# RMSNorm inside a two-layer decoder trunk: the sum of squares and its spread on TensorE, written another way

## The chip, the cores and the metric

The kernel runs on one core of a Trainium2 chip. The metric is device time in microseconds (us) of one execution; several runs are given, and one further execution was profiled. The engines are named as in the profile: PE (TensorE matmul), PEld (its weight loads), DVE (VectorE), ACT (ScalarE), POOL (GpSimd) and SP (SyncE).

## The reference

A trunk of two layers on x of shape (1, 1024, 1024) in float32: a gated short convolution with a SwiGLU FFN, then dilated attention with a SwiGLU FFN, then a last norm. What matters here is the norm, which is taken five times, over the model dimension:

```python
def rms_norm(x, g):
    xf = x.astype(jnp.float32)
    y = xf * lax.rsqrt(jnp.mean(xf * xf, axis=-1, keepdims=True) + EPS)
    return (y * g.astype(jnp.float32)).astype(x.dtype)

def reference(x, mix_norm, ffn_norm, final_norm, ...):
    for i in range(DEPTH):                       # DEPTH = 2
        h = rms_norm(x, mix_norm[i])
        if i % N_MIXERS == 0:
            x = x + short_conv_mixer(h, ...)
        else:
            x = x + dilated_attention_mixer(h, ...)
        h = rms_norm(x, ffn_norm[i])
        x = x + swiglu(h, w_gate[i], w_up[i], w_down[i])
    return rms_norm(x, final_norm)
```

## The kernel before, in words

**Layout.** Activations are kept transposed: x is eight tiles X[0] to X[7] of 128 model dimensions by 1024 positions. A sum over the model dimension is thus a sum over partitions and over the eight tiles. A norm's factor 1/rms is one number per position, and where a tile is multiplied by it, it must stand in all 128 partitions: that is the tile `rstd`, 128 by 1024, the same row in every partition.

**Products.** Every float32 product is made of three matmuls of a type called fp32r in the program (F32R): an operand is split into a high part (a Copy on ACT into an F32R tile) and a low part (a subtraction on DVE, line 144 in `split`, 565 for activations), and high times high, high times low and low times high are added in a PSUM bank. The weights are combined and split while the kernel runs (a Strassen scheme: sums of weight blocks, the "combos", line 191; seven products m = 1 to 7 per unit u). A unit's product is twelve matmuls of 512 columns, lines 572 to 574; the plain products are lines 371 to 373.

**Order.** The schedule is written by hand: each engine runs its instructions in the order in which the program emits them. After each product the program calls `start(n)` or a hook, and what is emitted there stands at that place in every engine's queue. `ensure(k)` emits the weight sums and splits up to the k-th operand; `combos[key, u](m)` emits weight sums alone. Small tiles of 512 columns come from a pool of 20 ("half pages", `half_page`).

**The norm.** `Norm` gathers squares of the X tiles in `acc` (128 by 1024, still to be summed over partitions). `stats(c0, c1)` is a generator in two steps. First step: for each 128 positions a plain float32 matmul with `acc` as weights and one column of ones gives the sums with positions on partitions (line 472); ACT takes a Sqrt (475), DVE a reciprocal (476), giving `r`, and DVE multiplies an identity by r into a diagonal tile of 512 columns (481). Second step: a plain float32 matmul of a tile of ones with the diagonal puts r in all partitions (488), and ACT copies the bank into `rstd` (489). The three callers:

- The convolution and the query and key projection (`mix`) take 1024 positions at once: the first step as `gather`, the second as `spread`, some units later. In the convolution the square of rstd is taken (1108) and applied on DVE (980). In the query and key projection `r` is kept for attention, where the value tiles are scaled by it with positions on partitions (1517).
- An FFN takes two halves of 512. The first belongs to `group1`, between the output tiles of the mixer's last product; the second is emitted in `start(n)` of `feed_forward`, the first step at n = key + 1 (key is 0 or 1 for the two FFNs), the second at n = key + 2. What follows is `second_half`, DVE's scaling of X by rstd (1278) and the splits of the result, and a small Silu (1366) that loads its table early.
- The last norm works in three pieces of 512, 256 and 256 positions, with its own `squared_sum` (1954, 1958, 1959, 1961) and `spread` (1969, 1982); the last piece's sum takes the last square as a term of its own (1956).

**Tables of ACT.** Sqrt, Silu, and Exp with Ln need different tables, and an ACT_TABLE_LOAD stands where the set changes. Some loads are put early by hand: a small Sqrt on a scratch tile at the end of attention (1695) and ahead of the last norm (1977), and a named set that holds Ln and Exp (LN_EXP) at the bias tables (530) and at attention's start (1812).

Of the kernel before, what the change touches and what calls it, by code (L numbers as in the profile page):

```python
# [17 lines left out]
S = 1024  # L18
# [81 lines left out]
def trunk(ctx: ExitStack, tc: tile.TileContext, x, gains_in, cwi, ck, cwo, wqkv, wo, relb,  # L100
# [24 lines left out]
    less = consts.tile([128, 5, KT], F32)  # L125
    taps = consts.tile([128, KT, 3], F32)
    ones = consts.tile([128, 128], F32)
    eye = consts.tile([128, 128], F32)
    eps = consts.tile([128, 1], F32)
    scratch = consts.tile([128, 1], F32)  # L130
# [265 lines left out]
    class Norm:  # L396
# [68 lines left out]
        def stats(self, c0, c1):  # L465

            self.flush()
            w = c1 - c0
            nt = w // 128
            b = bank()  # L470
            for t in range(nt):
                nc.tensor.matmul(b[:, t:t + 1], self.acc[:, c0 + 128 * t:c0 + 128 * t + 128], ones[:, 0:1],
                                 start=True, stop=True)
            r = self.r = consts.tile([128, KT], F32, name="r", tag="r", bufs=2)
            nc.scalar.activation(r[:, :nt], b[:, :nt], AF.Sqrt, scale=1.0 / D, bias=eps)
            nc.vector.reciprocal(r[:, :nt], r[:, :nt])
            diags = []
            for p0 in range(0, nt, 4):
                n = min(4, nt - p0)
                diag = half_page("diag")  # L480
                nc.vector.tensor_tensor(out=view(diag, 0, [[128, n], [1, 128]]),
                                        in0=view(eye, 0, [[0, n], [1, 128]]),
                                        in1=view(r, p0, [[1, n], [0, 128]]), op=ALU.mult)
                diags.append((c0 + 128 * p0, 128 * n, diag))
            yield
            for p0, n, diag in diags:
                b = bank()
                nc.tensor.matmul(b[:, :n], ones, diag[:, :n], start=True, stop=True)
                nc.scalar.activation(self.rstd[:, p0:p0 + n], b[:, :n], AF.Copy)

    def add_to_x(n, banks):
        for (c0, c1), b in banks.items():
# [377 lines left out]
    class Conv(Strassen):  # L870
# [182 lines left out]
        def mix(self, group1):  # L1053
# [48 lines left out]

            def gather():
                next(stats)

            def spread():
                run(stats)
# [14 lines left out]
    class QueryKey(Conv):  # L1122
# [43 lines left out]
        def mix(self):  # L1166
# [40 lines left out]

            def gather():
                next(stats)

            def spread():
                run(stats)
                self.ready = True

            def load():
# [21 lines left out]
    class Swiglu(Strassen):  # L1237
# [111 lines left out]
        def feed_forward(self, stats, last_step, after, final=None):  # L1349
            prep = []  # L1350

            def start(n):
                if n == 0:
                    last_step()
                    for m in (6, 7):
                        combos[self.key, 1](m)
                    ensure(self.at(3, 1))
                if n == self.key + 1:
                    next(stats)
                    combos[self.key, 2](6)  # L1360
                    ensure(self.at(0, 6))
                elif n == self.key + 2:
                    run(stats)
                    prep.append(self.second_half())
                    next(prep[0])
                    nc.scalar.activation(scratch, eps, AF.Silu)
                    ensure(self.at(1, 6))
                elif n == 4:
                    ensure(self.at(1, 7))
                elif n in (5, 7, 8, 10, 12):  # L1370
                    next(prep[0], None)
                if n in (8, 24):
                    self.ahead = 3 if n == 8 else 2

            self.run(start)
            key = ("d", self.key)
            if final:
                final(key, self.plain, self.hid)
                return
            for n in range(KT):  # L1380
                add_to_x(n, both(take(key + (n,), 2 if n > 3 else 1), self.plain, self.hid))
                after(n)
# [22 lines left out]
    def into_ffn(i, norm):  # L1405
# [10 lines left out]
        def group1(key, ks, acts):  # L1416
# [9 lines left out]
            def between(j, n):  # L1426
# [48 lines left out]
    def attention(norm, qk):  # L1475
# [193 lines left out]
        def finish(p):  # L1669
# [22 lines left out]
            yield  # L1692
            nc.scalar.activation(z[:, half(1)], z[:, half(1)], AF.Exp, scale=-1.0)
            scaled(1)
            nc.scalar.activation(scratch, eps, AF.Sqrt)
            yield
            last_part.append(rest)
            yield
# [110 lines left out]
                    add_to_x(n, {c: b})  # L1809

        X[:] = [None] * KT
        nc.scalar.preload_act_table_set(LN_EXP)
        bias = {0: load_bias(0)}
        load_kq(0)
        run(value_tiles(0, 0))
# [35 lines left out]


    nc.scalar.dma_start(gains, gains_in)

    def load_first():

# [53 lines left out]
    with tc.tile_pool(name="third", bufs=1) as scope["pool"]:  # L1910
# [5 lines left out]
        def final(key, ks, hid):  # L1916
# [55 lines left out]
            diags = []  # L1972

            def between(i, n):
                add_squares(int(n > 0))
                if (i, n) == (0, 5):
                    nc.scalar.activation(scratch, eps, AF.Sqrt)
                if i and n == 1:
                    diags.append(squared_sum(i - 1))
                elif i and n == 3:  # L1980
                    s = slice(*pieces[i - 1])
                    nc.scalar.activation(norm.rstd[:, s], spread(diags.pop()), AF.Copy)
# [67 lines left out]
```

## Time and profile before

| | |
|---|---|
| time, median of 3 runs | 2130.8 us (2130.04 to 2131.32) |
| time of the profiled execution | 2129.8 us |
| its span | 2128.0 us |
| granted TensorE clock, mean | 0.996 |
| PE busy | 2102.3 us (99%), 11082 matmuls |
| DVE busy | 1739.8 us (82%) |
| ACT busy | 1015.7 us (48%) |
| POOL busy | 234.4 us (11%) |

Times of the trace count from the span's start. A row of a timeline gives start, duration, engine, line, operation, tiles written and read, shapes and count; in brackets stands the idle time of the engine before it and what ended it. A float32 matmul that is not F32R has two records. Ends of matmuls are modelled, their starts are not, so PE's pace is read from one start to the next.

### The profile page before, as it was taken

What the parts mean: (1) busy time and instruction counts of PE and PEld (TensorE: products, weight loads), DVE (VectorE), ACT (ScalarE), POOL (GpSimd) and SP (SyncE); (2) the same over time, 40 slices, a digit from 0 to 9 for tenths busy, and PEclk for the clock granted to TensorE, in tenths of its full rate; (3) what the DMA queues carried; (4) which work ended last, traced back from release to release, by engine and by line L of the source; (5) the groups of instructions that cost most, each with busy time, mean ns of one, the idle gap of its engine ahead of it and who ended that gap; (6) DMA issues with size and microseconds to landing.
All of it is one profiled execution on the core that took longest, in us unless ns stands there. A gap on an engine that the chain in (4) does not pass through costs nothing.

```text
span 2128.0 us, 30922 instructions
## 1 busy us (share of the span) xinstructions
PE 2102.3 (99%) x11082; PEld 1806.5 (85%) x11082; DVE 1739.8 (82%) x3262; ACT 1015.7 (48%) x1861; POOL 234.4 (11%) x335
## 2 busy tenths in 40 slices
PE   9999999999999999999999999999999999999998
PEld 7888888888888888887899999888788888888887
DVE  8898769988888888878967687787998888888876
ACT  7333426443444554445545545554544444456435
POOL 1000000110101000010322322111011101001000
PEclk9999999999999999999999999999999999999999
DMA  7332642323333566351767767745223233358432
GB/s 219 94 94 70 228 134 75 104 100 109 114 101 108 162 208 211 108 168 40 250 208 186 182 182 211 216 164 152 64 85 109 101 108 114 105 195 241 157 95 79
DMA packets 141464, 300.78 MB, mean 141 GB/s; under 512 B 48188, under 2 KB 54414, under 8 KB 141312
## 3 DMA queue, kind: packets, MB, share of 16 engines
q1 hardware_dynamic: 107488, 201.94, 31.5%
q0 software_dynamic: 26192, 82.17, 11.9%
q10 hardware_dynamic: 7632, 14.70, 1.8%
q8 instruction: 88, 1.44, 0.3%
q14 instruction: 64, 0.52, 0.1%
HBM read 208.48 MB, written 82.93 MB: 137 GB/s over the span
## 4 chain that ended last, share of the span: by engine, by line
PE 85%; DVE 7%; ACT 3%; DMA 2%; issue 2%; POOL 1%; SPq 0%; DVEq 0%; ACTq 0%; POOLq 0%
PE bank L574 19%; PE bank L572 19%; PE bank L573 19%; PE bank L373 4%; PE bank L372 4%; PE bank L371 4%; PE bank L664 3%; PE bank L667 3%; PE bank L666 3%; PE bank L1642 2%; POOL mb L1623 1%; PE bank L1512 1%; PE bank L1513 1%; PE bank L1514 1%; DVE w L144 1%
## 5 line engine op out<-in xcount | busy, mean ns | idle before, releaser
L572 PE MATMUL bank<-b,w 128*128 128x512 f32 x1952 | 764.0, 391 | 2.2 <-ACT w L143 1.8
L574 PE MATMUL bank<-b,w 128*128 128x512 f32 x1952 | 762.0, 390 | 3.6 <-DVE w L144 3.5
L573 PE MATMUL bank<-b,w 128*128 128x512 f32 x1952 | 761.4, 390 | 0.4 <-DVE b L883 0.3
L574 PEld LDWEIGHTS bank<-b,w 128*128 128x128 f32 x1952 | 366.9, 188 | 83.9 <-DVE w L144 7.4
L572 PEld LDWEIGHTS bank<-b,w 128*128 128x128 f32 x1952 | 367.2, 188 | 78.9 <-ACT w L143 2.9
L573 PEld LDWEIGHTS bank<-b,w 128*128 128x128 f32 x1952 | 367.1, 188 | 76.3 <-DVE b L883 1.1
L143 ACT ACTIVATE w<-combo 128x512 fp32r<-128x512 f32 (+2 forms) x488 | 249.1, 540 | 230.2 <-DVE combo L191 213.3
L144 DVE TENSOR_TENSOR w<-combo,w 128x512 fp32r<-128x512 f32 (+2 forms) x488 | 277.7, 583 | 37.6 <-ACT w L143 36.9
L578 ACT ACTIVATE part<-bank 128x512 f32<-128x512 f32 x186 | 110.8, 596 | 390.0 <-PE bank L574 386.6
L144 DVE TENSOR_TENSOR w<-raw,w 128x512 fp32r<-128x512 f32 (+2 forms) x342 | 189.5, 576 | 37.5 <-ACT w L143 37.5
L582 DVE TENSOR_TENSOR part<-part,bank 128x256 f32<-128x256 f32 (+1 forms) x366 | 171.5, 500 | 31.1 <-PE bank L574 16.6
L143 ACT ACTIVATE w<-raw 128x512 fp32r<-128x512 f32 (+2 forms) x342 | 166.9, 530 | 44.4 <-PE bank L574 11.5
L371 PE MATMUL bank<-w_hi,w 128*128 128x512 f32 (+1 forms) x400 | 153.4, 384 | 3.8 <-ACT w_hi L143 3.7
L372 PE MATMUL bank<-w_lo,w 128*128 128x512 f32 (+1 forms) x400 | 149.8, 375 | 1.2 <-DVE w_lo L144 1.2
L373 PE MATMUL bank<-w_hi,w 128*128 128x512 f32 (+1 forms) x400 | 149.8, 375 | 0.7 <-DVE w L144 0.7
L493 DVE TENSOR_TENSOR x<-x,bank 128x512 f32<-128x512 f32 (+1 forms) x104 | 66.4, 644 | 62.6 <-PE bank L373 61.4
L802 DVE TENSOR_TENSOR x<-x,bank 128x512 f32<-128x512 f32 x136 | 93.2, 685 | 29.1 <-PE bank L574 29.1
L191 DVE TENSOR_TENSOR combo<-raw 128x512 f32<-128x512 f32 (+1 forms) x172 | 111.7, 649 | 0.0
L371 PEld LDWEIGHTS bank<-w_hi,w 128*128 128x128 f32 x400 | 75.8, 190 | 17.1 <-ACT w_hi L143 3.9
L372 PEld LDWEIGHTS bank<-w_lo,w 128*128 128x128 f32 x400 | 75.9, 190 | 14.9 <-DVE w_lo L144 2.0
L373 PEld LDWEIGHTS bank<-w_hi,w 128*128 128x128 f32 x400 | 75.6, 189 | 14.7 <-DVE w L144 1.6
L565 DVE TENSOR_TENSOR b<-hin,b 128x512 fp32r<-128x512 f32 x126 | 79.7, 689 | 9.3 <-ACT b L564 9.3
(243 smaller groups left out, 3467.1 us busy)
## 6 DMA issues: line engine op xcount, KB each, us to landing
hin<-part SPq DMA_DIRECT2D x126, 256.0 KB
raw<-in_ffn_w_gate SPq DMA_DIRECT2D x44, 512.0 KB
raw<-in_ffn_w_up SPq DMA_DIRECT2D x44, 512.0 KB
part<-sum POOLq DMA_DIRECT2D x72, 256.0 KB, 2.3
raw<-in_ffn_w_down SPq DMA_DIRECT2D x48, 384.0 KB
raw<-in_attn_w_qkv SPq DMA_DIRECT2D x27, 512.0 KB
raw<-in_conv_w_in SPq DMA_DIRECT2D x24, 512.0 KB
part<-part POOLq DMA_DIRECT2D x36, 256.0 KB, 2.4
```

The source lines that it names most:

```text
L143: nc.scalar.activation(hi, src, AF.Copy)
L144: eng.tensor_tensor(out=lo, in0=src, in1=hi, op=ALU.subtract)
L191: eng.tensor_tensor(out=c, in0=a, in1=b, op=op)
L371: nc.tensor.matmul(b, whi[:, a], ahi[:, s], start=first, stop=False)
L372: nc.tensor.matmul(b, whi[:, a], alo[:, s], start=False, stop=False)
L373: nc.tensor.matmul(b, wlo[:, a], ahi[:, s], start=False, stop=last)
L572: nc.tensor.matmul(b, hi[:, a], bhi, start=start and k == 0, stop=False, skip_group_check=True)
L573: nc.tensor.matmul(b, hi[:, a], blo, start=False, stop=False, skip_group_check=True)
L574: nc.tensor.matmul(b, lo[:, a], bhi, start=False, stop=k == n - 1, skip_group_check=True)
L578: nc.scalar.activation(t, b, AF.Copy)
L582: nc.vector.tensor_tensor(out=t, in0=t, in1=b, op=ALU.add)
L802: nc.vector.tensor_tensor(out=X[n][:, half(h)], in0=X[n][:, half(h)], in1=b, op=ALU.add)
```

## The change

The diff touches all norms but the last piece of the last one.

- `stats` becomes a generator of three steps: high parts of `acc` on ACT; low parts on DVE; then `spread_sums`, in which two F32R matmuls with a tile of ones (`ones_r`) as weights give the sum over partitions, in all partitions at once, and ACT takes Ln (with scale 1/D and eps) and Exp (with scale -1/2) into `rstd`.
- `gather` takes the first two steps at once. In the FFNs the first two steps are emitted with the two calls of `combos` (m = 6 and 7), so that the high parts stand ahead of one weight sum and the low parts behind it; for the second half this moves from n = key + 1 to n = 0.
- The value tiles' `r` is made by writing one row of `rstd` to DRAM and reading it back with positions on partitions, two DMAs on POOL's queue in the query and key projection's `spread`.
- The first two pieces of the last norm use `split` and `spread_sums`. The set LN_EXP is loaded at the start and ahead of the last norm; the loads at attention's start and end go; the Sqrt table is loaded behind the second piece's Exp for the last piece, which stays as it was.

```diff
@@ class Norm
         def stats(self, c0, c1):
 
             self.flush()
-            w = c1 - c0
-            nt = w // 128
-            b = bank()
-            for t in range(nt):
-                nc.tensor.matmul(b[:, t:t + 1], self.acc[:, c0 + 128 * t:c0 + 128 * t + 128], ones[:, 0:1],
-                                 start=True, stop=True)
-            r = self.r = consts.tile([128, KT], F32, name="r", tag="r", bufs=2)
-            nc.scalar.activation(r[:, :nt], b[:, :nt], AF.Sqrt, scale=1.0 / D, bias=eps)
-            nc.vector.reciprocal(r[:, :nt], r[:, :nt])
-            diags = []
-            for p0 in range(0, nt, 4):
-                n = min(4, nt - p0)
-                diag = half_page("diag")
-                nc.vector.tensor_tensor(out=view(diag, 0, [[128, n], [1, 128]]),
-                                        in0=view(eye, 0, [[0, n], [1, 128]]),
-                                        in1=view(r, p0, [[1, n], [0, 128]]), op=ALU.mult)
-                diags.append((c0 + 128 * p0, 128 * n, diag))
-            yield
-            for p0, n, diag in diags:
-                b = bank()
-                nc.tensor.matmul(b[:, :n], ones, diag[:, :n], start=True, stop=True)
-                nc.scalar.activation(self.rstd[:, p0:p0 + n], b[:, :n], AF.Copy)
+            parts = []
+            for p0 in range(c0, c1, HALF):
+                s = slice(p0, min(p0 + HALF, c1))
+                hi, lo = (half_page("sum", F32R) for _ in range(2))
+                nc.scalar.activation(hi, self.acc[:, s], AF.Copy)
+                parts.append((s, hi, lo))
+            yield
+            for s, hi, lo in parts:
+                nc.vector.tensor_tensor(out=lo, in0=self.acc[:, s], in1=hi, op=ALU.subtract)
+            yield
+            for s, *sums in parts:
+                spread_sums(self.rstd[:, s], sums)
+
+    def spread_sums(rstd, sums):
+        b = bank()[:, :rstd.shape[1]]
+        for i, t in enumerate(sums):
+            nc.tensor.matmul(b, ones_r, t, start=i == 0, stop=i == len(sums) - 1)
+        nc.scalar.activation(rstd, b, AF.Ln, scale=1.0 / D, bias=eps)
+        nc.scalar.activation(rstd, rstd, AF.Exp, scale=-0.5)
@@ Conv.mix and QueryKey.mix
             def gather():
                 next(stats)
+                next(stats)
@@ QueryKey.mix
             def spread():
                 run(stats)
+                rms = dram.tile([1, S], F32, name="rms")
+                norm.r = consts.tile([128, KT], F32, name="scales")
+                nc.gpsimd.dma_start(rms, norm.rstd[0:1, :])
+                nc.gpsimd.dma_start(norm.r, bass.AP(rms.tensor, rms.offset, [[1, 128], [128, KT]]))
                 self.ready = True
@@ Swiglu.feed_forward
                 if n == 0:
                     last_step()
                     for m in (6, 7):
+                        next(stats)
                         combos[self.key, 1](m)
                     ensure(self.at(3, 1))
                 if n == self.key + 1:
-                    next(stats)
                     combos[self.key, 2](6)
                     ensure(self.at(0, 6))
                 elif n == self.key + 2:
@@ into_ffn, group1
                 if n == i:
                     pre.append(norm.stats(0, HALF))
-                    next(pre[0])
                     for m in (6, 7):
+                        next(pre[0])
                         combos[i, 0](m)
@@ attention
-            nc.scalar.activation(scratch, eps, AF.Sqrt)
...
-        nc.scalar.preload_act_table_set(LN_EXP)
@@ the start
     nc.scalar.dma_start(gains, gains_in)
+    nc.scalar.preload_act_table_set(LN_EXP)
...
     nc.vector.memset(ones, 1.0)
+    nc.vector.memset(ones_r.bitcast(F32), 1.0)
@@ final
                 if (i, n) == (0, 5):
-                    nc.scalar.activation(scratch, eps, AF.Sqrt)
+                    nc.scalar.preload_act_table_set(LN_EXP)
                 if i and n == 1:
-                    diags.append(squared_sum(i - 1))
+                    s = slice(*pieces[i - 1])
+                    known.append(split(norm.acc[:, s], [half_page("sum", F32R)[:, :s.stop - s.start] for _ in range(2)]))
                 elif i and n == 3:
                     s = slice(*pieces[i - 1])
-                    nc.scalar.activation(norm.rstd[:, s], spread(diags.pop()), AF.Copy)
+                    spread_sums(norm.rstd[:, s], known.pop())
                     scale.extend((i - 1, k, norm.rstd[:, s]) for k in range(KT))
+                    if i == len(pieces) - 1:
+                        nc.scalar.preload_act_table(AF.Sqrt)
```

More of the change, by code (lines that the diff above doesn't have):

```diff
@@ L127, in trunk @@
     ones = consts.tile([128, 128], F32)
+    ones_r = consts.tile([128, 128], F32R)
     eye = consts.tile([128, 128], F32)
@@ L1355, in start @@
                     for m in (6, 7):
+                        next(stats)
                         combos[self.key, 1](m)
@@ L1970, in spread @@
                 return b[:, :w]
-            diags = []
+            known = []
             def between(i, n):
```

## The prediction, made before the changed kernel was run

> **What bounds the kernel now.** I read the page first, then busy time by stretch, then the timelines of PE, ACT and DVE around each of the five norms.
>
> ```profile
> span 2128.0 us, 30922 instructions
> PE 2102.3 (99%) x11082; PEld 1806.5 (85%) x11082; DVE 1739.8 (82%) x3262; ACT 1015.7 (48%) x1861; POOL 234.4 (11%) x335
> PE 85%; DVE 7%; ACT 3%; DMA 2%; issue 2%; POOL 1%; SPq 0%; DVEq 0%; ACTq 0%; POOLq 0%
> ...
> 352.00:400.00 48.00, 48.00 (x214) 39.76 (x213) 47.77 (x83) 26.91 (x48) 3.06 (x6) 1.00 0.25 82
> 1470.00:1520.00 50.00, 48.99 (x218) 39.99 (x217) 46.17 (x76) 33.77 (x59) 5.12 (x6) 1.00 0.30 74
> ```
>
> The first three lines are the span, the busy times and the chain's shares by engine: PE is busy 99% of the span and holds 85% of the chain. Less PE work therefore shortens the run wherever the engines that feed PE keep up. The two stretches (length, PE, PEld, DVE, ACT, POOL) show where that is in doubt: just behind the norm of each FFN, DVE is busy 47.77 of 48 and 46.17 of 50 us. The accounting is thus: PE time taken out, less what DVE and ACT cannot follow.
>
> **PE: what goes and what comes.** The norm of the convolution on PE's timeline, 1024 columns:
>
> ```profile
> 66.53 0.39 PE L574 MATMUL bank<-b,w 128*128 128x512 f32 x1
> 66.76 1.84 PE L472 MATMUL bank<-ones,acc 128*128 128x1 f32 x16
> ...
> 68.79 0.40 PE L573 MATMUL bank<-b,w 128*128 128x512 f32 x1
> ...
> 76.77 1.88 PE L488 MATMUL bank<-diag,ones 128*128 128x512 f32 x4
> ...
> 78.72 0.40 PE L573 MATMUL bank<-b,w 128*128 128x512 f32 x1
> ```
>
> Ends are modelled, so I go by starts. A 512-column matmul of high or low parts starts 0.23 us after the one before (66.53 to 66.76). The eight one-column products (sixteen records) hold PE from 66.76 until the L573 at 68.79, less the one L572 between, 68.79 - 66.76 - 0.23 = 1.80 us. The two fp32 spreads hold it 78.72 - 76.77 - 0.23 = 1.72 us. The new form has four products of high or low parts, 4 x 0.23 = 0.92 us (their type is that of L572, so I take that row's price). So 1.80 + 1.72 - 0.92 = 2.60 us of PE go per 1024 columns. Four norms have 1024 columns and the last one changes on 768: 4.75 x 2.60 = 12.4 us, the most that PE's work alone can give.
>
> **What ACT and DVE get.** Groups by line and form (busy us, mean ns):
>
> ```profile
> L143 ACT ACTIVATE w<-combo 128x512 fp32r<-128x512 f32 x248 | 150.9, 626 | 108.5 <-DVE combo L191 108.2
> L144 DVE TENSOR_TENSOR w<-combo,w 128x512 fp32r<-128x512 f32 x248 | 170.0, 688 | 30.9 <-ACT w L143 30.7
> L882 ACT ACTIVATE b<-x,gains 128x512 fp32r<-128x512 f32 x36 | 24.1, 717 | 36.1 <-DVE x L493 26.0 <-DMA oh<-in_one_hot 3.7 <-issue 3.2
> L1665 ACT ACTIVATE z<-bank 64x512 f32<-64x512 f32 x32 | 18.9, 591 | 17.4 <-PE bank L1642 16.9
> L1632 ACT ACTIVATE lp<-lp 128x512 f32<-128x512 f32 x16 | 9.8, 615 | 0.0
> L481 DVE TENSOR_TENSOR diag<-eye,r 128x512 f32<-128x512 f32 x8 | 5.4, 690 | 0.3
> L489 ACT ACTIVATE rstd<-bank 128x512 f32<-128x512 f32 x8 | 4.6, 596 | 10.4 <-PE bank L488 10.3
> ```
>
> Per 512 columns DVE exchanges the 0.69 us diagonal for a 0.69 us subtraction and loses a reciprocal: no dearer. ACT gets a high part (0.63), a Ln and an Exp (0.62) for a small Sqrt and a 0.60 copy. A Ln out of a bank with eps as operand isn't in the trace: L1665 without an operand is 0.59, L882 with one 0.72; I take 0.65, and about 0.06 more for Exp to wait for it. So rstd comes 0.73 us later behind its matmul than by the copy, in each half. ACT is 48% busy; this counts only where DVE waits for rstd.
>
> **Convolution: 2.6.** There DVE does wait:
>
> ```profile
> 77.83 0.60 ACT L489 ACTIVATE rstd<-bank 128x512 f32<-128x512 f32 x1 [4.09 <-PE bank L488]
> 80.41 0.69 DVE L980 TENSOR_TENSOR part<-part,acc 128x512 f32<-128x512 f32 x1 [2.75 <-ACT acc L1108]
> 87.15 0.39 PE L574 MATMUL bank<-b,w 128*128 128x512 f32 x1
> 82.35 0.69 DVE L144 TENSOR_TENSOR w<-combo,w 128x512 fp32r<-128x512 f32 x1
> ```
>
> PE reaches the spread 1.80 earlier and ends it 2.60 earlier; on ACT 2 x 0.73 = 1.46 us more stand ahead of L1108, so DVE resumes at least 1.1 earlier and loses at most 1.5 us on PE. The low part that ends at 82.35 + 0.69 is first read at 87.15, 4.1 us later: the lead covers it, and the whole 2.60 stays.
>
> **FFNs: 2.7 and 1.9.** The second half's norm, one row of FFN 0 (340), then FFN 1:
>
> ```profile
> 340.47 1.05 PE L472 MATMUL bank<-ones,acc 128*128 128x1 f32 x8 [0.24 <-DVE acc L446]
> ...
> 1493.87 1.02 PE L488 MATMUL bank<-diag,ones 128*128 128x512 f32 x2
> 1494.93 0.60 ACT L489 ACTIVATE rstd<-bank 128x512 f32<-128x512 f32 x1 [2.97 <-PE bank L488]
> 1495.56 2.50 DVE L1278 TENSOR_TENSOR x<-x,rstd 128x512 f32<-128x512 f32 x4 [1.25 <-ACT rstd L489]
> 1518.17 0.50 PE L574 MATMUL bank<-b,w 128*128 128x512 f32 x1 [1.01 <-DVE w L144]
> ```
>
> In FFN 1, PE reaches the spread earlier by the first half's 1.30 and the one-column products' 0.90: at 1491.67 instead of 1493.87. Two matmuls end about 0.6 later (second start, and its 0.39), at 1492.3; Ln and Exp give rstd at 1493.6, and DVE begins its scaling 1.9 us earlier than 1495.56. From there to 1518.17, where PE waited 1.01 us for a low part, DVE has work throughout: the 1470 to 1520 row leaves it 3.8 us idle in all, 1.25 of them in the row at 1495.56 itself and the rest ahead of it. PE would be there 2.6 earlier, DVE 1.9: the wait grows to 1.7, and 1.9 stays. High and low parts are now asked for at n = 0, two or three units ahead of the spread, so it finds them made; their subtraction stands behind one weight sum on DVE so that DVE doesn't stand idle for ACT's high part. FFN 0 runs the same list but its spread comes one unit earlier, twelve matmuls or 2.7 us: at the same place it has 2.7 - 1.01 = 1.7 us to spare, and the 352 to 400 row shows no idle PE. It loses 0.7 of that and keeps 2.6, with some 0.1 of the 0.24 us in which PE waited for the squares' sum.
>
> **Query and key: 1.9.**
>
> ```profile
> 981.97 1.28 ACT L475 ACT_TABLE_LOAD   x1
> 983.26 0.27 ACT L475 ACTIVATE r<-bank,eps 128x8 f32<-128x8 f32 x1
> 996.40 0.60 ACT L578 ACTIVATE part<-bank 128x512 f32<-128x512 f32 x1 [2.13 <-PE bank L574]
> 997.55 0.69 DVE L144 TENSOR_TENSOR w<-combo,w 128x512 fp32r<-128x512 f32 x1 [0.72 <-ACT w L143]
> 1001.89 0.60 ACT L578 ACTIVATE part<-bank 128x512 f32<-128x512 f32 x1 [1.67 <-issue]
> 1003.13 1.41 DVE L883 SCALAR_TENSOR_TENSOR b<-x,gains,b 128x512 fp32r<-128x512 f32 x2 [1.15 <-ACT b L882]
> 1019.04 0.50 PE L574 MATMUL bank<-b,w 128*128 128x512 f32 x1 [0.47 <-DVE w L144]
> ```
>
> At 1019.04 PE waits for DVE, which has worked without a pause since 1003.13. So what counts is how much earlier DVE comes. Its two pauses of 0.72 and 1.15 lie behind ACT copies (L578) that waited for PE; with PE 2.6 earlier both go, 1.87 together. The two ACT operations more at the spread (1.3 us) use room that the lost table load and earlier matmuls make ahead of it. I keep 1.9 of 2.6.
>
> **1/rms by way of DRAM.** Two DMAs are new on POOL's queue, and the second waits for the first. No row has 4-byte pieces, so their price is open upwards:
>
> ```profile
> part<-sum POOLq DMA_DIRECT2D x72, 256.0 KB, 2.3
> 1019.41 0.58 POOL L1146 DMA_DIRECT2D kq<-kq_hi  x1 [74.22 <-ACT w L143]
> 1093.34 1.28 ACT L1812 ACT_TABLE_LOAD   x1
> 1094.63 0.84 ACT L1517 ACTIVATE v<-bank,r 128x256 f32<-128x256 f32 x2
> ```
>
> By the first row (2.3 us from issue to landing) with 0.58 an issue, two in series are about 6 us. rstd is made ahead of the copy at 996.40; the first issue behind them on POOL comes at 1019.41, the first reader at 1094.63. Up to 23 us nothing stands behind them: nothing lost. Without that cover the key stores would wait, and with them attention's first loads.
>
> **Table loads.** The loads for the first and the third norm's Sqrt (981.97), at attention's start (1093.34) and at its end go; the one ahead of the last norm becomes one of Ln and Exp, and a Sqrt load is added ahead of the last piece. The row at 981.97 prices one at 1.28: the Sqrt starts 0.01 us behind its end. PE's waits name none of them, so they are worth nothing beyond what is counted here. The Trainium skill, "ScalarE: Activation LUTs", What ACT_TABLE_LOAD costs, gives about 2.66 us for a switch, drain included. The trace shows no such drain around the load (0.01 us). By that page the added load alone would be 1.38 dearer, an estimate, and the time about 2122.3.
>
> **The end: 0.8.**
>
> ```profile
> 2113.87 0.36 ACT L1982 ACTIVATE rstd<-bank 128x256 f32<-128x256 f32 x1
> 2115.06 0.42 ACT L1929 ACTIVATE sq<-x 128x256 f32<-128x256 f32 x1 [0.82 <-DVE x L493]
> 2118.45 0.42 ACT L1929 ACTIVATE sq<-x 128x256 f32<-128x256 f32 x1 [0.43 <-DVE x L493]
> ```
>
> 768 columns give PE 1.95, 1.30 of it ahead of this place. ACT then does Ln, Exp and a load where one copy stood: about 0.4 + 1.28 = 1.7 more. Free at 2114.23 before, it is free at 2114.23 - 1.30 + 1.7 = 2114.6; the squares of tiles 4 to 7 start 0.45 earlier than 2115.06 and, without the last 0.43 us of waiting, the last one 0.8 earlier. What follows it is unchanged.
>
> **Sum.** 2.6 + 2.7 + 1.9 + 1.9 + 0.8 = 9.9 us. The profiled run took 2129.8 us (span 2128.0 and 1.8 around it); it would take 2119.9 and span 2118.1. The runs' median, 2130.8, is 1.0 above it: **2120.9 us**. Attention gets no term: its waits follow from what arrives, and all of that arrives earlier alike. A small shift there is in the range.
>
> **Rivals.** (1) *All of PE's time carries*: DVE's leads are longer than the waits show. 12.4 gives 2118.4. For it: behind the convolution and FFN 0 PE shows no wait. Against it: at 1019 and 1518 it waits already, so there the lead is nil. (2) *ACT and DVE bind*: Ln and Exp come late at both FFNs and the table load holds the end. Convolution 2.0, FFNs 1.5 and 1.0, query and key 0.9, end 0.0: 5.4, 2125.4. For it: DVE's 47.77 of 48. (3) *The change doesn't get one table set*: Ln and Exp each load theirs, 2 x 1.28 more per spread. FFN 1 and the query and key lose 2.6 each, FFN 0 0.9 beyond its spare 1.7, the end 1.5: 2.3 left, 2128.5. Against it: attention's Exp and Ln (L1632, L1665) alternate through the slots behind L1812's one load. (4) *Slower: the pool of 20 half tiles runs full.* At an FFN's start there are 8 scaled columns, 8 weight sums, 2 saved products and 1 diagonal, 19 by the code; two parts for one diagonal make 20. A high part that must wait for a tile holds everything behind it on ACT, copies out of banks too, and PE then waits for a product's end, 2.7 us. At both halves of both FFNs, the convolution and the query and key that is 6 x 2.7 = 16.3 against 9.9: 2137.3. It decides from four places on. Against it: 20 still fit, and elsewhere there are fewer tiles. (5) *The added Sqrt load holds ACT for twice its 1.28 us*: the last square is then 0.5 late in place of 0.8 early, 8.6, 2122.2. Against it: the 0.01 us behind the load at 981.97.
>
> **How the numbers follow.** Forecast 0.64 (own range 2119 to 2122.5), rival 1 0.14, rival 2 0.11, rival 3 0.03, rival 4 0.05, rival 5 0.03. About 0.2% (4.3 us) is what a measurement here tells from none: faster by more is the forecast with rivals 1, 2 and 5, 0.92; within it is rival 3, 0.03; slower is rival 4, 0.05. The range goes from 2117.2 (rival 1 with a microsecond for attention) to 2125.4 (rival 2).
>
> **What would show it.** L472 and L488 gone from PE and PE's busy time about 12 us less; PE's wait near 1518 grown to about 1.7 and that near 1019 to about 1.2; no new PE wait in the convolution and behind FFN 0's norm; six ACT table loads instead of nine, no two within one norm; the value tiles never waiting for a DMA. Wrong would be: a PE wait at the new products themselves, ACT waiting at a high part for a tile, or PE waits behind the norms that sum to over 5 us.

## The result, and the profile after

| | before | changed |
|---|---|---|
| median of 5 runs | 2130.8 us (2129.76 to 2131.7) | 2121.44 us (2121.1 to 2122.22) |
| ratio, 95% interval | | 0.9957 [0.9946, 0.9968] |
| profiled execution | 2129.8 us, span 2128.0 | 2121.1 us, span 2119.3 |

The change makes the kernel 9.4 us faster by the medians and 8.7 by the two profiled executions; the forecast was 9.9 and 2120.9 us. A second measurement of the changed kernel gave 2121.37 us, 0.9959 [0.9946, 0.9971].

The page's first lines and the two stretches behind the FFNs' norms, for the changed kernel (length, PE, PEld, DVE, ACT, POOL):

```profile
span 2119.3 us, 30767 instructions
PE 2088.8 (99%) x11006; PEld 1795.5 (85%) x11006; DVE 1737.2 (82%) x3255; ACT 1023.0 (48%) x1868; POOL 236.5 (11%) x337
352.00:400.00 48.00, 48.00 (x213) 39.75 (x212) 47.90 (x84) 26.94 (x50) 4.25 (x8) 1.00 0.27 94
1470.00:1520.00 50.00, 48.47 (x212) 39.48 (x212) 48.83 (x81) 33.81 (x59) 3.94 (x5) 1.00 0.30 75
```

PE is busy 13.5 us less (11.5 less in a second profile of the changed kernel, 2090.8 us), and the span is 8.7 shorter. The two stretches are the same in time, not in work: the changed kernel is 5.4 us ahead at the first and 8.6 us at the second. Behind FFN 0's norm PE is still busy throughout. Behind FFN 1's it now stands idle for 1.53 us and DVE has only 1.17 left.

**A table by stage.** The products are the same in all kernels here, so the same product on PE can be found in two traces and its starts compared. The difference at the end of a stage less that at its start is what the stage costs more than in the changed kernel. Columns are us against the changed kernel's first profile; stages are bounded by its times. The last two columns part the last norm at the start of PE's last product (2107.29).

| profile | up to 64 | convolution, to 110 | FFN 0, 300 to 400 | query, key, 930 to 1060 | attention, to 1440 | FFN 1, to 1600 | 2070 to last product | from there to the end |
|---|---|---|---|---|---|---|---|---|
| before | -0.20 | 2.71 | 2.93 | 2.03 | -0.13 | 1.91 | 1.21 | -1.69 |
| changed, again | 0.61 | 0.00 | 0.06 | -0.04 | -0.22 | -0.05 | -0.05 | -0.01 |

The stretches left out differ by 0.05 at most. The second row shows how to read the table: in the stages with a norm two profiles of one program agree within 0.06 us; the first 64 us and attention vary from execution to execution. So does the closing wait, from the end of DVE's last scaling to the end of the span: 3.57 us in the changed kernel, 3.62 in its second profile, 3.21 in the kernel before, and 3.16 in a kernel below whose last norm is the changed one's. Of the -1.69, -0.36 is this wait and no work of the norm.

Forecast against measured: 2.6 and 2.71, 2.7 and 2.93, 1.9 and 2.03, 1.9 and 1.91, and at the end 0.8 against 1.21 - 1.69 = -0.48, or -0.12 without the closing wait.

**Where it comes from.** The convolution's norm on PE's timeline:

```profile
74.90 0.39 PE L572 MATMUL bank<-b,w 128*128 128x512 f32 x1
75.12 1.07 PE L485 MATMUL bank<-sum,ones_r 128*128 128x512 f32 x4
76.03 0.39 PE L570 MATMUL bank<-b,w 128*128 128x512 f32 x1
```

Four products from 75.12 to 76.03: 0.91 us, the forecast's 0.92; no PE wait follows. PE's waits at the other norms that are new, or that the forecast named:

```profile
339.38 0.50 PE L485 MATMUL bank<-sum,ones_r 128*128 128x512 f32 x1 [0.30 <-DVE sum L477]
...
979.30 0.39 PE L571 MATMUL bank<-b,w 128*128 128x512 f32 x1
979.79 0.50 PE L572 MATMUL bank<-b,w 128*128 128x512 f32 x1
...
1011.59 0.50 PE L572 MATMUL bank<-b,w 128*128 128x512 f32 x1 [0.64 <-DVE w L145]
...
1501.72 0.50 PE L570 MATMUL bank<-b,w 128*128 128x512 f32 x1 [0.45 <-ACT part L576]
...
1508.99 0.50 PE L572 MATMUL bank<-b,w 128*128 128x512 f32 x1 [1.08 <-DVE w L145]
```

The last is the wait that stood at 1518.17 before, with 1.01. It grew by 0.07 only; the other 0.45 that PE lost came one unit earlier, at a product whose bank ACT had not yet emptied. The third of a microsecond at 339.38 is new: PE waits at the norm's own second product for the low part. Ahead of the query and key norm's spread, the product at 979.79 starts 0.49 us behind the one before it instead of 0.23; in the kernel before, the same two start 0.23 apart.

Groups by line and form (busy us, mean ns, idle time ahead and what ended it), the value tiles' reader last:

```profile
L486 ACT ACTIVATE rstd<-bank,eps 128x512 f32<-128x512 f32 x9 | 6.1, 681 | 6.8 <-PE bank L485 6.7
L487 ACT ACTIVATE rstd<-rstd 128x512 f32<-128x512 f32 x9 | 5.7, 635 | 0.3
...
L1521 ACT ACTIVATE v<-bank,scales 128x256 f32<-128x256 f32 x32 | 14.7, 469 | 33.9 <-PE bank L1518 30.6 <-issue 3.2
```

POOL's two new DMAs on its timeline, with the key store behind them:

```profile
988.20 0.49 POOL L1215 DMA_DIRECT2D rms<-rstd  x1 [48.38 <-ACT b L562]
990.07 0.95 POOL L1216 DMA_DIRECT2D scales<-rms  x1 [1.38 <-DMA rms<-rstd]
1010.58 0.57 POOL L1145 DMA_DIRECT2D kq<-kq_hi  x1 [19.56 <-ACT kq_hi L1144]
```

Ln took 0.68 us and Exp 0.635, where 0.65 and 0.62 were assumed. Both DMAs are issued within 2.8 us, POOL's next work comes 19.56 us later, and what ends the value tiles' waits is PE, never a DMA.

**The end is where the forecast failed.** DVE and PE at the last norm, before:

```profile
2096.84 0.18 DVE L1959 RECIPROCAL r<-r 128x4 f32<-128x4 f32 x1 [1.18 <-ACT r L1958]
...
2100.94 0.69 DVE L1940 TENSOR_TENSOR x<-x,rstd 128x512 f32<-128x512 f32 x1 [1.18 <-ACT rstd L1982]
...
2110.09 0.17 DVE L1959 RECIPROCAL r<-r 128x2 f32<-128x2 f32 x1 [1.17 <-ACT r L1958]
...
2114.27 0.42 DVE L1940 TENSOR_TENSOR x<-x,rstd 128x256 f32<-128x256 f32 x1 [1.01 <-ACT rstd L1982]
...
2117.99 0.42 DVE L493 TENSOR_TENSOR x<-x,bank 128x256 f32<-128x256 f32 x1 [0.29 <-PE bank L373]
2118.80 0.27 PE L1954 MATMUL bank<-ones,acc 128*128 128x1 f32 x1 [0.85 <-DVE acc L1936]
```

and in the changed kernel:

```profile
2088.05 0.69 DVE L145 TENSOR_TENSOR sum<-acc,sum 128x512 fp32r<-128x512 f32 x1 [1.55 <-ACT sum L144]
2092.20 0.69 DVE L1944 TENSOR_TENSOR x<-x,rstd 128x512 f32<-128x512 f32 x1 [2.12 <-ACT rstd L487]
2100.95 0.42 DVE L145 TENSOR_TENSOR sum<-acc,sum 128x256 fp32r<-128x256 f32 x1 [1.39 <-ACT sum L144]
2105.48 0.42 DVE L1944 TENSOR_TENSOR x<-x,rstd 128x256 f32<-128x256 f32 x1 [1.56 <-ACT rstd L487]
2105.46 1.28 ACT L1990 ACT_TABLE_LOAD   x1
2106.76 0.42 ACT L1933 ACTIVATE sq<-x 128x256 f32<-128x256 f32 x1
2108.89 0.42 DVE L491 TENSOR_TENSOR x<-x,bank 128x256 f32<-128x256 f32 x1
2109.70 0.27 PE L1958 MATMUL bank<-ones,acc 128*128 128x1 f32 x1 [2.12 <-DVE acc L1940]
```

Before, DVE's last sum into x (2117.99) waited for PE. Now PE's last product starts at 2107.29, and DVE comes to that sum 1.6 us later, without a pause ahead of it: DVE has fallen behind PE. It stands idle four times, 6.6 us in all, at each low part and each first scaling; before, the same two pieces cost it 4.5 us, at each reciprocal and each first scaling. What PE saves there is given back at PE's next wait, 2.12 instead of 0.85.

### The profile page after: what moved, and what is told of

It is laid out like the page before. It is cut to its first block, busy times and chain, and to the rows that moved or that the text cites. A ratio compares the mean times of both kernels' runs of the same rounds, so it can differ in the third digit from the quotient of the medians.

```text
span 2119.3 us, 30767 instructions
## 1 busy us (share of the span) xinstructions
PE 2088.8 (99%) x11006; PEld 1795.5 (85%) x11006; DVE 1737.2 (82%) x3255; ACT 1023.0 (48%) x1868; POOL 236.5 (11%) x337
## 4 chain that ended last, share of the span: by engine, by line
PE 45%; DVE 5%; ACT 2%; issue 1%; POOL 1%; DMA 0%; SPq 0%; DVEq 0%; ACTq 0%; POOLq 0%
PE bank L572 8%; PE bank L570 8%; PE bank L571 8%; PE bank L1646 4%; PE bank L373 2%; PE bank L374 2%; PE bank L372 2%; PE bank L662 1%; PE bank L665 1%; PE bank L664 1%; PE bank L1516 1%; PE bank L1517 1%; PE bank L1518 1%; PE bank L1574 1%; PE bank L1573 1%
```

## The experiments

Each kernel is the changed one but for the edit shown. The medians are of runs beside the kernel before (2129.95 to 2130.76 us in these sets); the changed kernel itself ran in the first measurement and beside the last three kernels. The stages are read as above. Three dots in an edit stand for lines that are not shown.

**One norm old at a time.** In the old form `stats` is that of the kernel before, with its steps at their old places; for query and key the two DMAs go and the table load at attention's start comes back.

```diff
- stats = norm.stats(0, S)          # convolution; likewise FFNs; query, key
+ stats = norm.stats_old(0, S)
...
```

> The changed kernel with the convolution's norm in its old form (one-column float32 products, Sqrt, reciprocal, diagonal, float32 spread); every other norm in the new form; its Sqrt brings one ACT table load more. The forecast (term 2.6): 2.6 us above the changed kernel's 2121.4, so 2124.0. All PE time carries: 2.6 too. ACT and DVE bind (rival 2): 2.0, 2123.4. In the trace the gain over the kernel before, taken at the same product on PE, should be about 0 behind the convolution's spread, where the changed kernel stands 2.64 further.

> The changed kernel with the norms of both FFNs in their old form and at their old places (first step ahead of the two weight sums, for the second half at n = key + 1); the others new. The forecast (terms 2.7 and 1.9): 4.6 us above the changed kernel, 2126.0; in the trace 2.7 of it is lost by FFN 0 and 1.9 by FFN 1, where PE's wait ahead of the unit behind the norm should fall. All PE time carries: 5.2, 2.6 in each. ACT and DVE bind: 1.5 and 1.0, 2.5 in all, 2123.9.

> The changed kernel with the query and key projection's norm in its old form, so without the two DMAs for r and with the table loads that its Sqrt and attention's Exp then need; the others new. The forecast (term 1.9): 1.9 us above the changed kernel, 2123.3, lost by about 1020 us. All PE time carries: 2.6, 2124.0. ACT and DVE bind: 0.9, 2122.3. If the way by DRAM or attention cost something after all, it would be below 1.9.

| profile | median | up to 64 | convolution | FFN 0 | query, key | attention | FFN 1 |
|---|---|---|---|---|---|---|---|
| convolution old | 2128.92 | 2.11 | 2.71 | 3.99 | -0.08 | 0.81 | -0.07 |
| FFNs old | 2129.51 | 0.40 | 0.00 | 4.15 | -0.01 | -0.13 | 2.46 |
| query, key old | 2122.4 | -0.16 | 0.03 | 0.03 | 2.09 | -0.22 | -0.02 |

Query and key: 2.09, close to the forecast's 1.9 and to 2.03 before; the way by DRAM costs nothing (attention -0.22, as in the changed kernel's second profile). The median lies only 1.0 above; the profiled execution, 1.3 above, gives the rest back in the first 64 us, in attention and in the closing wait (3.16 us instead of 3.57). The other two medians are 7.5 and 8.1 above, far over any theory, and neither test is clean: both kernels load ACT tables where neither the kernel before nor the changed one does. With the convolution old, FFN 0 loses 3.99 us although its own norms are new: a Sqrt now precedes, and Ln and Exp then load a table each. With the FFNs old, the Sqrt meets the wrong table inside the norm. ACT's and DVE's timelines of the latter:

```profile
312.91 1.28 ACT L476 ACT_TABLE_LOAD   x1
314.50 0.18 DVE L477 RECIPROCAL r<-r 128x4 f32<-128x4 f32 x1 [2.27 <-ACT r L476]
```

**The same without the stray loads.** Convolution and FFNs old, and the small Sqrt back at attention's end:

```diff
+ nc.scalar.activation(scratch, eps, AF.Sqrt)    # attention, as before
```

> The changed kernel with the norms of the convolution and of both FFNs in their old form and at their old places, and with the small Sqrt back at attention's end, so that no Sqrt and no Ln meets a wrong table inside an FFN's norm; query and key and the end stay new. The forecast's terms: 2.6 + 2.7 + 1.9 = 7.2 above the changed kernel's 2121.4, so 2128.6. All PE time carries: 7.8, 2129.2. ACT and DVE bind: 4.5, 2125.9. If the excess of the two kernels before (7.5 with the convolution's norm old, 8.1 with the FFNs' old) was not their table loads but that each new norm needs its neighbours new, it stays over 10 above. In the trace, the gain over the kernel before at the same product should stay near 0 up to 1480 us.

Stages: convolution 2.71, FFN 0 2.93, FFN 1 1.92, each within 0.01 of the kernel before. So with the right tables these three norms are worth the same whether the query and key norm and the last one are old or new. The median, 2131.58 (2129.23 to 2133.78), is however 10.1 above the changed kernel, where the stages give 7.6. The profiled execution is the longest of the eleven. It has 2.32 us in the first 64 us, 1.81 in attention, 0.30 in the query and key stage, and 0.71 behind PE's last product, where the last one-column products start 0.38 to 0.43 us apart instead of 0.22 to 0.24. The shortest execution lies 7.8 above the changed kernel's median. What of that is chance and what belongs to the program is taken up at the end.

**Tables.** The line that loads Ln's and Exp's set at the start is taken out:

```diff
- nc.scalar.preload_act_table_set(LN_EXP)
```

> The changed kernel without the one line that loads the set LN_EXP at the start. If Ln and Exp then each load a table of their own until the bias tables load the set (936 us): four loads in the convolution's norm, two in each half of FFN 0's, none in the later norms. By the forecast's rival 3 as worked out there (2.6 of later rstd per half against the spare of the place): convolution 4 x 1.28 = 5.1 less the 2.6 of lead that is left, 2.5; FFN 0 0.9; 2124.8. By what the kernel with the convolution's norm old showed in FFN 0 (4.0 lost): 2.5 + 4.0 = 6.5, 2127.9. If ACT's loads were hidden as ACT is 48% busy: 0, 2121.4.

2128.97 us, 7.5 above; ratio to before 0.9993 [0.9984, 1.0002]: one line carries most of the gain. Convolution 3.19, FFN 0 3.95, 7.1 together; no later norm changes. ACT in the convolution's norm:

```profile
76.61 0.69 ACT L486 ACTIVATE rstd<-bank,eps 128x512 f32<-128x512 f32 x1 [2.38 <-PE bank L485]
77.32 1.28 ACT L487 ACT_TABLE_LOAD   x1
78.61 0.63 ACT L487 ACTIVATE rstd<-rstd 128x512 f32<-128x512 f32 x1
79.26 1.28 ACT L486 ACT_TABLE_LOAD   x1
80.56 0.69 ACT L486 ACTIVATE rstd<-bank,eps 128x512 f32<-128x512 f32 x1
81.27 1.28 ACT L487 ACT_TABLE_LOAD   x1
```

This is rival 3, and it is dearer than the 0.9 that it gave FFN 0. The Trainium skill, "ScalarE: Activation LUTs", Table sets: the hidden batching unit, names a set that holds both functions, so that Ln and Exp in turn need one load. With the line the trace agrees: no load stands between them. Without it the rows above differ: each brings its own, so in this kernel the common set has to be asked for by name.

**The order in the FFNs undone.** Low parts right behind high parts, for the second half both at n = key + 1:

```diff
                     for m in (6, 7):
-                        next(stats)
                         combos[self.key, 1](m)
...
                 if n == self.key + 1:
+                    next(stats)
+                    next(stats)
...
+                    next(pre[0])
+                    next(pre[0])
                     for m in (6, 7):
-                        next(pre[0])
                         combos[i, 0](m)
```

> The changed kernel with the order in the FFNs undone: low parts right behind the high parts with no weight sum between, and for the second half both at the old place, n = key + 1 in place of n = 0. The forecast's step says that the order keeps DVE from standing idle for the high part: without it DVE waits 0.6 us in each half; FFN 1 has no lead and loses 0.6, FFN 0 at most as much: 2122.0 to 2122.6. Rival: DVE stands idle 1.9 us for rstd right behind it anyway, and the later place takes away PE's 0.30 us wait for the low part in FFN 0: no change or 0.3 less, 2121.1 to 2121.4.

2125.95 us, 4.5 above; FFN 0 1.88, FFN 1 0.75, 2.6 by the stages. The step holds: in the first half of each FFN DVE waits 1.22 us for the high part, twice what was expected. FFN 0 loses three times what was expected: PE now reaches the second half's products before their parts are made. Order and place are undone together here, so what each is worth alone is not shown.

```profile
312.71 0.69 DVE L477 TENSOR_TENSOR sum<-acc,sum 128x512 fp32r<-128x512 f32 x1 [1.22 <-ACT sum L473]
...
339.12 0.51 PE L485 MATMUL bank<-sum,ones_r 128*128 128x512 f32 x1 [0.64 <-ACT sum L473]
340.88 0.50 PE L485 MATMUL bank<-sum,ones_r 128*128 128x512 f32 x1 [1.25 <-DVE sum L477]
```

**1/rms later.**

```diff
                 spread_sums(self.rstd[:, s], sums)
+                for _ in range(2):
+                    nc.scalar.activation(self.rstd[:, s], self.rstd[:, s], AF.Copy)
```

> The changed kernel with two further Copies of rstd onto itself behind each Exp, so rstd comes about 1.25 us later in each half (2.5 at the end of a 1024-column norm), the last norm left alone. By the forecast's steps: convolution 0 (lead 4.1, of which the change used 1.5), FFN 0 0.3 (1.0 left of its spare 1.7), FFN 1 1.25 (no lead), query and key 0 to 1.2: 1.5 to 2.7 above, 2122.9 to 2124.1, and PE's wait near 1509 grown from 1.08 to 2.3. All PE time carries (leads longer than the waits show): 0, 2121.4.

2130.67 us: 9.2 above, the whole gain. Convolution 1.89, FFN 0 2.17, query and key 2.63, FFN 1 2.10. Both theories had far more room behind the norms than there is. In FFN 0 PE waits 0.53 and 0.77 us for the second half's high and low part, in the query and key stage 0.81 and 1.24 for low parts of weights. In the convolution and FFN 1:

```profile
94.36 0.50 PE L572 MATMUL bank<-b,w 128*128 128x512 f32 x1 [1.23 <-DVE part L582]
...
1510.88 0.50 PE L572 MATMUL bank<-b,w 128*128 128x512 f32 x1 [1.77 <-ACT part L578]
1518.15 0.50 PE L574 MATMUL bank<-b,w 128*128 128x512 f32 x1 [1.08 <-DVE w L145]
```

The wait for a low part in FFN 1 did not grow (1.08, as in the changed kernel). At the other two PE waits not for an operand, where the prediction measured the lead, but for a bank: the product starts only when DVE or ACT has read what stood there. The convolution's bank, before and in the changed kernel:

```profile
91.60 0.68 DVE L582 TENSOR_TENSOR part<-part,bank 128x512 f32<-128x512 f32 x1
94.85 0.39 PE L572 MATMUL bank<-b,w 128*128 128x512 f32 x1
...
90.70 0.68 DVE L580 TENSOR_TENSOR part<-part,bank 128x512 f32<-128x512 f32 x1
92.35 0.39 PE L570 MATMUL bank<-b,w 128*128 128x512 f32 x1
```

Before, PE starts 2.6 us behind the end of DVE's read; in the changed kernel 1.0 us of room is left. At the low part that the prediction took, the lead is 4.1 us before and 2.5 after.

**The last norm old.**

```diff
-                    nc.scalar.preload_act_table_set(LN_EXP)
+                    nc.scalar.activation(scratch, eps, AF.Sqrt)
                 if i and n == 1:
...
-                    known.append(split(norm.acc[:, s], [half_page("sum", F32R)[:, :s.stop - s.start] for _ in range(2)]))
+                    diags.append(squared_sum(i - 1))
...
-                    spread_sums(norm.rstd[:, s], known.pop())
+                    nc.scalar.activation(norm.rstd[:, s], spread(diags.pop()), AF.Copy)
...
-                        nc.scalar.preload_act_table(AF.Sqrt)
```

> The changed kernel with the last norm's first two pieces in their old form (no Ln, no Exp, no table load behind them); the four other norms new. The forecast (term 0.8): 0.8 us above the changed kernel, 2122.2. All PE time carries: 1.95 above, 2123.4. What the two traces say now, that DVE and not PE sets the pace behind the first piece's norm and that it waits longer for Ln and Exp than it did for Sqrt, diagonal and copy (2.12 and 1.56 against 1.18 and 1.01 us): 0.5 to 1.0 below, 2120.4 to 2120.9, with PE's last product later but the last Sqrt earlier than in the changed kernel.

2121.36 us, no change; the stage is 1.21 - 1.29 = -0.08. The forecast's 0.8 and all of PE's 1.95 are ruled out. The expected gain of 0.5 to 1.0 isn't there either: the change is worth nothing at this place.

**Why, and a better end.** First the Sqrt load alone is taken away: the last piece's r by Ln and Exp. Then the steps are set one tile apart. Then the last piece, too, loses diagonal and spread.

```diff
# no load
-                nc.scalar.activation(r[:, :nt], b[:, :nt], AF.Sqrt, scale=1.0 / D, bias=eps)
-                nc.vector.reciprocal(r[:, :nt], r[:, :nt])
+                nc.scalar.activation(r[:, :nt], b[:, :nt], AF.Ln, scale=1.0 / D, bias=eps)
+                nc.scalar.activation(r[:, :nt], r[:, :nt], AF.Exp, scale=-0.5)
...
-                        nc.scalar.preload_act_table(AF.Sqrt)
# order
...
-                if i and n == 1:
...
-                    known.append(split(norm.acc[:, s], [half_page("sum", F32R)[:, :s.stop - s.start] for _ in range(2)]))
-                elif i and n == 3:
...
-                    spread_sums(norm.rstd[:, s], known.pop())
+                if i and n == 0:
+                    known.append([half_page("sum", F32R)[:, :s.stop - s.start] for _ in range(2)])
+                    nc.scalar.activation(known[0][0], norm.acc[:, s], AF.Copy)
+                elif i and n == 1:
+                    nc.vector.tensor_tensor(out=known[0][1], in0=norm.acc[:, s], in1=known[0][0], op=ALU.subtract)
+                elif i and n == 2:
+                    spread_sums(norm.rstd[:, s], known.pop())
+                elif i and n == 3:
                     scale.extend((i - 1, k, norm.rstd[:, s]) for k in range(KT))
# last piece
-            diag = squared_sum(last, sums.pop()[0])
...
+            nc.tensor.matmul(b, ones, norm.acc[:, s], start=True, stop=False)
+            nc.tensor.matmul(b, ones, sums.pop()[0][:, s], start=False, stop=True)
...
+            nc.scalar.activation(rstd, b, AF.Ln, scale=1.0 / D, bias=eps)
+            nc.scalar.activation(rstd, rstd, AF.Exp, scale=-0.5)
             some(KT)
-            rstd = spread(diag)
```

> The changed kernel once more, unaltered, beside the three below on one chip. If it is fixed in all its stages, 2121.1 to 2122.2 as before, and a profile whose stages differ from its first by under 0.1 us; what still differs (the first 64 us, attention) is chance, and tells how far single profiles of the other kernels may be read there.

> The changed kernel without the Sqrt table load behind the second piece: the last piece's 1/rms, 128 x 2, by Ln and Exp in place of Sqrt and reciprocal. By the forecast's step for the end (ACT's 1.28 us load and its Ln and Exp delay the last squares): 0.8 to 1.3 below, 2120.1 to 2120.6. By the trace, where DVE has three operations a tile behind it and ACT only makes up its delay: 0.1 to 0.2 below, 2121.2.

> The same, and the last norm's steps one tile apart: high part with tile 0 of the next piece, low part with tile 1, products, Ln and Exp with tile 2, scaling from tile 3 on (before: high and low part together with tile 1, the rest with tile 3). If DVE's four idle stretches (1.55, 2.12, 1.39 and 1.56 us) set the end, most of them go, the last sum into x follows PE's last product (2107.3) at once and not 1.6 later: 1.2 to 1.6 below the kernel without the load, about 2119.8. If the end is set by ACT or by the last chain alone: no change.

> The same again, and the last piece's sum by two float32 products of the tile of ones with acc and with the last square, straight into all partitions, then Ln and Exp of 128 x 256, in place of one-column products, 1/rms, diagonal and spread. Two float32 matmuls of 256 columns (0.5 us at the end, one of them ahead of the last square) with 0.46 and 0.42 of ACT stand where 0.5 of one-column products, 0.26 + 0.17, 0.42 of diagonal and 0.5 of spread stood with two hand-overs more: 0.7 to 1.1 below the kernel before it, about 2118.9, and faster than both kernels.

| profile | median | ratio to before | 2070 to last product | from there to the end |
|---|---|---|---|---|
| changed, again | 2121.37 | 0.9959 [0.9946, 0.9971] | -0.05 | -0.01 |
| no load | 2121.28 | 0.9957 [0.9945, 0.997] | -0.03 | -0.06 |
| and order | 2119.44 | 0.9947 [0.9935, 0.996] | -0.67 | -1.24 |
| and last piece | 2118.67 | 0.9944 [0.993, 0.9957] | -0.67 | -2.57 |

The load costs nothing: without it ACT stands idle 0.82 us ahead of the next square, while DVE keeps its idle stretches (2.11 and 1.55) and its pace. Taking DVE's pauses away gives 1.8, and DVE again waits for PE ahead of its last sum. The last piece gives another 1.33, of which 0.19 is the closing wait. The last kernel:

```profile
2107.78 0.42 DVE L491 TENSOR_TENSOR x<-x,bank 128x256 f32<-128x256 f32 x1 [0.35 <-PE bank L374]
2108.59 0.70 PE L2003 MATMUL bank<-acc,ones 128*128 128x256 f32 x2 [0.85 <-DVE acc L1940]
2109.12 0.59 PE L2004 MATMUL bank<-sq,ones 128*128 128x256 f32 x2
2109.76 0.47 ACT L2006 ACTIVATE rstd<-bank,eps 128x256 f32<-128x256 f32 x1 [0.57 <-PE bank L2004]
2110.26 0.42 ACT L2007 ACTIVATE rstd<-rstd 128x256 f32<-128x256 f32 x1
2110.71 2.77 DVE L1944 TENSOR_TENSOR x<-x,rstd 128x256 f32<-128x256 f32 x8 [0.84 <-ACT rstd L2007]
```

By its stages this kernel is 3.2 us below the changed one, by the medians 2.7; it is the fastest of all, 0.56% below the kernel before. The intervals of neighbouring rows overlap; the steps between them are read from the stages.

## Why the prediction was right, point by point

- **PE's work.** Right: 12.4 was put as the most, and PE's busy time fell by 13.5, by 11.5 against the second profile of the changed kernel. In the FFNs, with their single groups of 512 columns, it was somewhat more than 2.60: at FFN 1's spread PE stood 2.7 ahead of where it entered the stage.
- **Convolution 2.6.** The sum was right (2.71), its reason only in part: the lead that was measured, 4.1 us at a low part, isn't the shortest. At a bank read by DVE it was 2.6. The change used 1.6 of it, near the 1.5 forecast, and 1.0 is left. So the step held because this lead, which the prediction hadn't looked at, was long enough too; the kernel with the later 1/rms shows where it ends.
- **FFN 0, 2.7.** Right (2.93), with a reason as loose: 1.0 us was said to remain of its spare time, and 1.25 us more of latency in each half cost 2.17. What was missed is that rstd of the first half delays DVE up to the last square, and with it the second half's low part (339.38). That wait at a new product is one of the prediction's signs of being wrong; it came, but with 0.30 us.
- **FFN 1, 1.9.** Right in size and mechanism. DVE's scaling moved from 1495.56 to 1486.38, 9.18, of which 7.28 came in from the stages ahead: 1.9, as forecast. PE's loss was put at 0.7 in one wait near 1518. It lost 0.8 (2.7 less 1.91), but 0.45 of it at ACT's copy and only 0.07 more at that wait; the rest is in the first starts behind the pauses.
- **Query and key 1.9.** 2.03 and 2.09. The wait was to grow from 0.47 to 1.2 and is 0.64: DVE came 2.1 earlier where 1.9 was forecast. PE's loss is near the 0.7 forecast all the same, for 0.4 of it stands at 979.79, ahead of the spread, where the forecast had no wait.
- **Order of the parts.** Right, and under-sized: together with the place it holds 1.88 + 0.75.
- **1/rms by DRAM.** Nothing, as said; the pair takes 5 us (988.20 to the second's landing, 3.1 behind its issue at 990.07), where 6 were estimated.
- **Table loads.** Six instead of nine, none between a Ln and its Exp. The added one takes 1.28 us, 2105.46 to the next square at 2106.76, and the kernel without it is no faster (2121.28): rival 5 is ruled out. The Trainium skill, "ScalarE: Activation LUTs", What ACT_TABLE_LOAD costs, gives 2.66 us with drain; no drain shows here.
- **The end, 0.8.** Wrong by 0.9, by 1.3 with the closing wait. The failed step is that ACT, free at 2114.6, would set the last squares: ACT's load makes no difference. DVE sets them, and its pauses, which the step didn't look at, grew by 0.9 and 0.55 at the two scalings and stand at 1.55 and 1.39 for the low parts, where the reciprocals had 1.18 and 1.17.
- **Rivals.** The first, all PE time, is ruled out in FFN 1, the query and key and the end; the second by every term but its 0.0 at the end; the fourth's waits of 2.7 us are nowhere, the longest behind a norm of the middle stages is 1.08, and no high part waits for a tile. The third is what happens when the load at the start is missing.

The sum came out so close partly by luck: the end's miss of 0.9 stood against 0.5 by which the four other terms together were too small.

## What to carry to other kernels

Measure a lead at everything that the next unit waits for, its PSUM banks before its operands: here the bank's lead was 2.6 us where the operand's was 4.1. A cheaper form on the bound engine pays only where its feeders' order follows it: the same arithmetic was worth nothing at the end until its steps were set one tile apart, and then 1.8 us. When two functions share a table set, one early load of that set can be most of the gain (7.5 of 9.4 here), and a test that puts one old piece back must put its tables back too.

## What the runs showed of the hardware

PE's granted clock, by stretches of 15 us, in the kernel with the old convolution norm:

```profile
20.00:35.00 15.00, 12.61 (x54) 9.81 (x54) 14.17 (x23) 11.89 (x20) 1.78 (x2) 1.00 0.46 133
50.00:65.00 15.00, 12.78 (x49) 9.81 (x48) 13.29 (x21) 4.67 (x8) 0.00 (x0) 0.89 0.48 141
```

For 2 to 3.4 us, once at most in the first 65 us, matmuls of 512 columns start every 0.43 us instead of 0.23. In six of the fourteen profiles this follows PE's pauses near 27 us; by the pause near 59 four of these have made it up, and two still lie 0.8 and 1.0 us behind. In two it follows the pause near 59 and costs about 1.6 us, the 2.11 of the table with 0.5 brought in. In six it doesn't show.

The longest of these pauses is 2.22 us. The Trainium skill, "TensorE: Matmul & The Clock Gate", Part 1: The HAM clock gate, tells of a clock that falls to half after an idle window of about 3.4 us; the windows run free of the kernel. The half speed agrees; the pauses here are shorter than that.

Attention's spread, -0.22 to 1.81, arises between 1100 and 1200 us. Both of the kernels with the slow stretch near 59 have the old convolution norm. Whether that form brings it on, and with it the 2.5 us that the median of the three old norms lies above its stages, stays open. So does the 1.9 of the kernel with the order undone, whose profiled execution (2124.06) is among its lowest (2123.52 to 2127.33).
